# A value head's high and low parts side by side in one TensorE operand: weighing the values in a banded attention, in a two-layer transformer kernel

## The chip, the cores and the metric

One core of a Trainium2 chip runs the kernel as a single program. The metric is the device time of one execution in microseconds (us), median over runs. The engines are named as in the profile: PE (TensorE, matrix products; PEld is its weight load), DVE (VectorE), ACT (ScalarE), POOL (GpSimd) and SP (the queue that issues most DMAs). Each engine works through its own list of instructions in order; an instruction waits on semaphores for what it needs from other engines.

## The reference

Two layers on 512 tokens of width 1024, all in float32. Layer 0 has a differential attention, layer 1 a banded one; each layer ends in a gated feed-forward network. The change lies in the banded attention of layer 1:

```
def swa_sink_attention(h, cos, sin, w_q, q_norm, sinks, w_o, kw, vw):
    ...
    s = jnp.einsum('bnqhgd,bnkhd->bnhgqk', qb, kw).astype(jnp.float32) * (1.0 / math.sqrt(HEAD_DIM))
    ...
    m = jnp.maximum(jnp.max(s, axis=-1, keepdims=True), sink)
    e = jnp.exp(s - m)
    p = e / (jnp.sum(e, axis=-1, keepdims=True) + jnp.exp(sink - m))
    o = jnp.einsum('bnhgqk,bnkhd->bnqhgd', p.astype(vw.dtype), vw)
    return o.reshape(B, S, SW_HEADS * HEAD_DIM) @ w_o
```

There are 4 blocks of 128 queries, 4 value heads of 64 columns, and 4 query heads for each value head. A block of queries sees its own block of keys and the one before it; the first block has only its own.

## The kernel before

**Split products.** TensorE takes rounded operands (the type fp32r), so every float32 operand is split into a high part (a rounding cast on ACT, `split_evac` L298 or `split` L585) and a low part (the difference, on DVE, L299 or L587). `mm3` (L291 to L294) makes a product from three matmuls: high by high, high by low and low by high.

**Stages.** Pairs of heads of layer 0's attention, its feed-forward network (to about 605 us in the profile), the banded attention (about 605 to 785 us), the second feed-forward network (to the end). The order of PE's instructions is the order in which the program calls them (`manual_schedule` for PE). The other engines' orders come from a scheduler that works with priorities: `tc.high_priority` with a larger offset puts instructions forward.

**The banded attention.** It has 16 units, one for each block of queries and value head. A unit goes through `turn_q` (transpose the queries), `score` (products with the keys into two PSUM banks; DVE takes mask and maximum, L1388; ACT takes the exponentials, L1399, and scales them, L1406), `turn_p` (four transposes per key block on PE, L1418, then the split of the probabilities into `ph` on ACT, L298, and `pl` on DVE, L299) and `weigh`, the step that changes. When each step of a unit is issued on PE stands in a table written by hand, `SW_AT` (L117, five numbers per unit); between two steps, `Fill` puts in matmuls of the dense products that are due then (the projections of the queries, keys and values, later the output projection `o_sw`). This table is the same in both kernels.

**weigh before (L1424 to L1439).** The probabilities of a key block stand as 512 columns: 256 for the two even query heads, 256 for the two odd ones. The values lie in two padded tensors, `vpad[0]` (high) and `vpad[1]` (low), with 64 columns of zeros on either side of each head's 64. For the even heads the operand is taken so that the 64 value columns come first and zeros second, for the odd heads the other way round, and both are added into the same 256 columns of one PSUM bank `po`: partitions 0 to 63 hold the even heads and 64 to 127 the odd ones. Per key block that is 2 halves of `mm3`, six matmuls over 256 columns. Four units have one key block, twelve have two: 28 blocks. `po` then leaves through `split_evac` (L1438): ACT casts `oh` from PSUM, DVE subtracts `ol` from PSUM. There is one buffer for `po`, so the next unit's first matmul waits until both have read it. `oh` and `ol` are the operands of the output projection. The zeros of `vpad` are written once on POOL (two memsets, L1294), ahead of the rotation tables that POOL makes for this stage.

Of the kernel before, what the change touches and what calls it, by code (L numbers as in the profile page):

```python
# [17 lines left out]
P = 128  # L18
S = 512
NT = S // P  # L20
# [117 lines left out]
def tile_yoco_hybrid(  # L138
# [27 lines left out]
    def nm(s):  # L166
        count[0] += 1
        return f"{s}_{count[0]}"
# [1103 lines left out]
    with tc.tile_pool(name="sw", bufs=1, reuse_waits="tile") as ap:  # L1272
# [7 lines left out]
        maskS = maskD[:, 256:512]  # L1280
        vpad = [ap.tile([P, NT, 9, HD], F32R, name=nm("vpad"), tag=f"vpad{e}") for e in range(2)]
        kT = new_kT(ap, "kTs")
# [4 lines left out]
        def prepare():  # L1287
# [4 lines left out]
                                    compare_op=ALU.is_gt, fill=NEG, base=0, channel_multiplier=-1)  # L1292
            for e in range(2):
                nc.gpsimd.memset(vpad[e][:, :, 0::2, :].bitcast(F32), 0.0)  # L1294
            tables(Cs, Ss, gsw, HD, nc.gpsimd, nc.gpsimd)
# [35 lines left out]
        def b_post(pts):  # L1331

            ts["B"] = []
            for t in range(NT):
# [4 lines left out]
                src = heads(pts[t][:, 256:512])  # L1339
                dh = vpad[0][:, t, 1::2, :]  # L1340
                with tc.high_priority(offset=HOT):
                    nc.scalar.activation(dh, src, AF.Copy, scale=rx[:, t:t + 1])
                    nc.vector.scalar_tensor_tensor(vpad[1][:, t, 1::2, :], src, rx[:, t:t + 1], dh.bitcast(F32),
                                                   op0=ALU.mult, op1=ALU.subtract)
# [79 lines left out]
        def weigh(u):  # L1424
            s, i, kk, kv, blocks = place(u)
            nb = len(blocks)
            po = att("po")
            assert vdone
            for b, blk in enumerate(blocks):
                for e in range(2):  # L1430
                    c0 = (2 * kv + 1 - e) * HD
                    vf = [vpad[z][:, blk].rearrange("p a e -> p (a e)")[:, c0:c0 + P] for z in range(2)]
                    es = slice(e * 256, (e + 1) * 256)
                    mm3(po[:, 0:256], vf[0], vf[1], pT[u, b][0][:, es], pT[u, b][1][:, es],
                        b == 0 and e == 0, b == nb - 1 and e == 1)
            oh = ap.tile([P, 2, P], F32R, name=nm("oh"), tag="oh", bufs=OSW)
            ol = ap.tile([P, 2, P], F32R, name=nm("ol"), tag="ol", bufs=OSW)
            split_evac(oh, ol, po[:, 0:256].rearrange("p (h q) -> p h q", q=P))  # L1438
            o_all[kv, i] = (oh, ol)  # L1439
# [106 lines left out]
```

## Time and profile before

| what | value |
|---|---|
| three runs | 1122.22, 1124.5 and 1125.8 us, median 1124.5 us |
| the profiled execution, span from first to last instruction | 1121.8 us |
| granted TensorE clock over the whole span | 1.000 of full speed |
| PE busy over the span | 1101.6 us, 98% |
| DVE busy | 1008.4 us, 90% |
| ACT busy | 711.3 us, 63% |

The span is the profiled execution's own time; what lies around it isn't recorded. The median of the runs is 2.7 us above it.

A busy share is an average over stages. Views that show one stretch (busy time by windows, the timeline, the chain of waits) say which engine the others wait for in it. In the chain, each piece is the work that the next piece waited for, with the share of the time that no other work hides.

### The profile page before, as it was taken

The numbers are of one execution on the slowest core, as the hardware profiler recorded it, in microseconds if no ns is written. First come the engines' busy times: TensorE is split into PE (matmuls) and PEld (weight loads), VectorE is DVE, ScalarE is ACT, GpSimd is POOL, SyncE is SP. The second block draws the span as 40 slices with busy tenths as digits, with TensorE's granted clock in tenths as the row PEclk, the third lists the DMA queues.
The fourth block names the chain that finished last, engine by engine and source line by source line (L and its number), as shares of the span: only waits on it lengthen the run. The fifth ranks groups of instructions, "written<-read, shape, count | busy, mean of one in ns | idle before, by whom it ended". The sixth has DMA issues, their size and how long they took to land.

```text
span 1121.8 us, 20162 instructions
## 1 busy us (share of the span) xinstructions
PE 1101.6 (98%) x7206; PEld 978.3 (87%) x7206; DVE 1008.4 (90%) x2418; ACT 711.3 (63%) x1577; POOL 55.5 (5%) x76
## 2 busy tenths in 40 slices
PE   8999999999999999999999999999999999999998
PEld 6878888778989989989998778878989989998997
DVE  5979798979999899999998787988899999899997
ACT  6575756454555665675678499697555666566574
POOL 1100000000000010010003000000010000000000
PEclk9999999999999999999999999999999999999999
DMA  6312121124453434336124311120545247246213
GB/s 198 113 57 77 38 77 50 65 72 140 146 162 98 141 80 160 112 82 203 57 48 106 111 41 57 39 76 25 198 138 168 76 104 207 85 104 178 77 30 103
DMA packets 94085, 114.90 MB, mean 102 GB/s; under 512 B 5993, under 2 KB 70914, under 8 KB 93986
## 3 DMA queue, kind: packets, MB, share of 16 engines
q1 hardware_dynamic: 87216, 100.97, 28.1%
q0 software_dynamic: 6720, 12.65, 6.3%
q8 instruction: 56, 0.92, 0.3%
q14 instruction: 43, 0.35, 0.1%
q10 hardware_dynamic: 50, 0.01, 0.0%
HBM read 99.98 MB, written 2.10 MB: 91 GB/s over the span
## 4 chain that ended last, share of the span: by engine, by line
PE 77%; DVE 12%; ACT 6%; DMA 2%; issue 1%; SPq 1%; DVEq 0%; ACTq 0%
PE acc L721 16%; PE tr L721 10%; PE tr L809 9%; PE acc L809 8%; PE acc L292 8%; PE acc L294 8%; PE acc L293 8%; PE po L721 2%; PE tr L435 2%; ACT s L1399 2%; DVE hss L385 1%; ACT s L1406 1%; DVE lo L587 1%; DMA r<-in_w_gate_up_dram 1%; PE tr L310 1%
## 5 line engine op out<-in xcount | busy, mean ns | idle before, releaser
L585 ACT CAST hi<-r 128x512 fp32r<-128x512 f32 x160 | 98.9, 620 | 79.5 <-PE acc L721 35.8
L292 PE MATMUL acc<-hi,hTh 128*128 128x512 f32 (+1 forms) x352 | 132.9, 377 | 2.5 <-DVE vl L1022 1.4
L293 PE MATMUL acc<-lo,hTh 128*128 128x512 f32 (+1 forms) x352 | 124.1, 353 | 0.4 <-DVE lo L269 0.4
L294 PE MATMUL acc<-hi,hTl 128*128 128x512 f32 (+1 forms) x352 | 124.2, 353 | 0.1
L585 ACT CAST hi<-g 128x512 fp32r<-128x512 f32 x154 | 94.9, 618 | 40.8 <-PE acc L293 19.2
L587 DVE TENSOR_TENSOR lo<-r,hi 128x512 fp32r<-128x512 f32 x160 | 105.3, 692 | 6.1 <-ACT hi L585 5.8
L585 ACT CAST hi<-raw 128x512 fp32r<-128x512 f32 x108 | 66.9, 621 | 62.5 <-PE tr L721 18.2
L792 ACT CAST ah<-lf 128x256 fp32r<-128x256 f32 x154 | 61.1, 404 | 47.9 <-PE tr L809 16.0
L721 PE MATMUL acc<-hTh,lo 128*128 128x256 f32 x288 | 81.6, 283 | 0.0
L721 PE MATMUL acc<-hTl,hi 128*128 128x256 f32 x288 | 81.5, 283 | 0.0
L721 PE MATMUL acc<-hTh,hi 128*128 128x256 f32 x288 | 81.5, 283 | 0.0
L721 PE MATMUL acc<-tl,hi 128*128 128x256 f32 x288 | 81.2, 282 | 0.0
L721 PE MATMUL acc<-th,hi 128*128 128x256 f32 x288 | 81.1, 282 | 0.0
L721 PE MATMUL acc<-th,lo 128*128 128x256 f32 x288 | 81.1, 282 | 0.0
L268 ACT CAST hi<-raw 128x512 fp32r<-128x512 f32 x96 | 57.3, 619 | 33.9 <-PE acc L294 24.6
L292 PEld LDWEIGHTS acc<-hi,hTh 128*128 128x128 f32 x352 | 66.7, 190 | 13.4 <-issue 2.6
L587 DVE TENSOR_TENSOR lo<-g,hi 128x512 fp32r<-128x512 f32 x110 | 76.1, 692 | 1.5 <-ACT hi L585 1.4
L294 PEld LDWEIGHTS acc<-hi,hTl 128*128 128x128 f32 x352 | 66.5, 189 | 10.1 <-DVE hTl L907 0.7
L584 POOL DMA_DIRECT2D lo<-g x44 | 38.5, 976 | 716.4 <-ACT lo L583 372.3
L587 DVE TENSOR_TENSOR lo<-raw,hi 128x512 fp32r<-128x512 f32 x108 | 73.4, 692 | 0.0
L269 DVE TENSOR_TENSOR lo<-raw,hi 128x512 fp32r<-128x512 f32 x96 | 64.7, 688 | 9.4 <-ACT hi L268 8.9
L293 PEld LDWEIGHTS acc<-lo,hTh 128*128 128x128 f32 x352 | 66.9, 190 | 6.5 <-DVE lo L269 0.7
(280 smaller groups left out, 3644.7 us busy)
## 6 DMA issues: line engine op xcount, KB each, us to landing
r<-in_w_gate_up_dram SPq DMA_DIRECT2D x80, 512.0 KB, 5.0
g<-in_w_down_dram SPq DMA_DIRECT2D x88, 256.0 KB, 5.4
lo<-g POOLq DMA_DIRECT2D x44, 256.0 KB, 3.8
raw<-in_da_w_qkv_dram SPq DMA_DIRECT2D x30, 256.0 KB, 3.3
raw<-in_da_w_qkv_dram SPq DMA_DIRECT2D x8, 512.0 KB, 3.7
raw<-in_da_w_o_dram SPq DMA_DIRECT2D x8, 512.0 KB, 3.7
raw<-in_w_gate_up_dram SPq DMA_DIRECT2D x8, 512.0 KB, 3.7
raw<-in_sw_w_o_dram SPq DMA_DIRECT2D x8, 512.0 KB, 3.8
```

The source lines that it names most:

```text
L268: nc.scalar.copy(hi, part)
L269: nc.vector.tensor_tensor(lo, part, hi.bitcast(F32), op=ALU.subtract)
L292: nc.tensor.matmul(dst, sh, mh, start=start, stop=False)
L293: nc.tensor.matmul(dst, sh, ml, start=False, stop=False)
L294: nc.tensor.matmul(dst, sl, mh, start=False, stop=stop)
L435: nc.tensor.matmul(banks[c][:, cols], q[a][rows], k[b][rows], start=a + b == 0, stop=a == 1)
L584: nc.gpsimd.dma_start(out=lo.bitcast(F32), in_=src, accum_op=ALU.add)
L585: nc.scalar.copy(hi, src)
L587: nc.vector.tensor_tensor(lo, src, hi.bitcast(F32), op=ALU.subtract)
L721: nc.tensor.matmul(dst, l[:, k, :], r[:, k, :], start=fresh and k == 0 and i == 0, stop=k == 3 and i == 2, skip_group_check=not fresh)
L792: nc.scalar.copy(ah, src)
L809: nc.tensor.matmul(bank, l[:, tk], r, start=fresh and i == 0 and n == 0, stop=i == len(qs) - 1 and n == 2, skip_group_check=not fresh)
```

## The change

The two padded tensors become one, `vv`, in which the 64 columns of a head's high part and the 64 of its low part stand side by side: 128 columns with no zeros. `weigh` takes this as the one operand, and streams all 512 columns of the high probabilities past it, then all 512 of the low ones: two matmuls per key block, in place of six. `po` now fills a whole bank: partitions 0 to 63 hold the sums with the high part, 64 to 127 those with the low part, and the columns hold the even heads and then the odd ones. (The product low by low, which `mm3` leaves out, is now in the sum.)

Since a head's two halves lie on different partitions, they are added behind the matmuls: ACT copies the lower half (64 partitions, 512 columns) to SBUF as `ocor`, and DVE adds it to the upper half in two additions of 256 columns into `osum`, the first for partitions 0 to 63 (even heads), the second for partitions 64 to 127 (odd heads). The split into `oh` and `ol` then reads `osum` in SBUF. `po` is free when the second addition has read it. `osum` and `ocor` have two buffers each. The two memsets on POOL are gone.

```diff
-        vpad = [ap.tile([P, NT, 9, HD], F32R, name=nm("vpad"), tag=f"vpad{e}") for e in range(2)]
+        vv = ap.tile([P, NT, 4, 2, HD], F32R, name=nm("vv"), tag="vv")
...
-            for e in range(2):
-                nc.gpsimd.memset(vpad[e][:, :, 0::2, :].bitcast(F32), 0.0)
...
-                dh = vpad[0][:, t, 1::2, :]
+                dh = vv[:, t, :, 0, :]
...
-                    nc.vector.scalar_tensor_tensor(vpad[1][:, t, 1::2, :], src, rx[:, t:t + 1], dh.bitcast(F32),
+                    nc.vector.scalar_tensor_tensor(vv[:, t, :, 1, :], src, rx[:, t:t + 1], dh.bitcast(F32),
...
             for b, blk in enumerate(blocks):
-                for e in range(2):
-                    c0 = (2 * kv + 1 - e) * HD
-                    vf = [vpad[z][:, blk].rearrange("p a e -> p (a e)")[:, c0:c0 + P] for z in range(2)]
-                    es = slice(e * 256, (e + 1) * 256)
-                    mm3(po[:, 0:256], vf[0], vf[1], pT[u, b][0][:, es], pT[u, b][1][:, es],
-                        b == 0 and e == 0, b == nb - 1 and e == 1)
+                v = vv[:, blk, kv].rearrange("p z e -> p (z e)")
+                for z in range(2):
+                    nc.tensor.matmul(po, v, pT[u, b][z], start=b == 0 and z == 0, stop=b == nb - 1 and z == 1)
...
-            split_evac(oh, ol, po[:, 0:256].rearrange("p (h q) -> p h q", q=P))
+            osum = ap.tile([P, 256], F32, name=nm("osum"), tag="osum", bufs=2)
+            ocor = ap.tile([P, 512], F32, name=nm("ocor"), tag="ocor", bufs=2)
+            with tc.high_priority(offset=pri["evac"]):
+                nc.scalar.copy(ocor[0:HD, :], po[HD:P, :])
+                for e in range(2):
+                    es = slice(e * 256, (e + 1) * 256)
+                    nc.vector.tensor_tensor(osum[e * HD:(e + 1) * HD, :], po[0:HD, es], ocor[0:HD, es], op=ALU.add)
+            split_evac(oh, ol, osum.rearrange("p (h q) -> p h q", q=P))
```

How the instructions stand on PE around the first unit's `weigh`, before. `acc` is a bank of a dense product, `tr` a bank of scores, and `po` the bank of the weighed values:

```order
L294 MATMUL acc_8354<-hi_8319,hTl_7565 128x512
L292 MATMUL po_8398<-ph_8167,vpad_7623 128x256
L293 MATMUL po_8398<-pl_8168,vpad_7623 128x256
L294 MATMUL po_8398<-ph_8167,vpad_7624 128x256
L292 MATMUL po_8398<-ph_8167,vpad_7623 128x256
L293 MATMUL po_8398<-pl_8168,vpad_7623 128x256
L294 MATMUL po_8398<-ph_8167,vpad_7624 128x256
L435 MATMUL tr_8411<-kTs_7625,q_8382 128x256
```

The same place on PE in the changed kernel:

```order
L294 MATMUL acc_8351<-hi_8316,hTl_7565 128x512
L1430 MATMUL po_8395<-ph_8164,vv_7623 128x512
L1430 MATMUL po_8395<-pl_8165,vv_7623 128x512
L435 MATMUL tr_8409<-kTs_7624,q_8379 128x256
L435 MATMUL tr_8410<-kTs_7624,q_8379 128x256
```

Six matmuls over 256 columns have become two over 512, and what stands around them on PE has not moved; this holds at all 28 blocks.

The end of the stage on ACT, before. `oh_9883` and `oh_9929` belong to the last two units, `hi` is a cast of feed-forward weights, `hTh` a cast of the transposed tokens of the feed-forward network, `xn` the squares for its norm:

```order
L522 ACTIVATE xn_9889,fss_9888<-xs 128x1024
L298 CAST ph_9866<-tr_9861 128x512
L298 CAST oh_9883<-po_9870 128x256
L298 CAST ph_9912<-tr_9907 128x512
L298 CAST oh_9929<-po_9916 128x256
L268 CAST hi_10010<-raw_10008 128x512
L268 CAST hi_10014<-raw_10008 128x512
L298 CAST hTh_9615<-tr_9940 128x4x128
L298 CAST hTh_9615<-tr_9947 128x4x128
```

The same place on ACT in the changed kernel (`oh_9846` and `oh_9889` are the last two units'):

```order
L298 CAST ph_9837<-tr_9832 128x512
L522 ACTIVATE xn_9857,fss_9856<-xs 128x1024
L1436 COPY ocor_9849<-po_9841 64x512
L298 CAST ph_9880<-tr_9875 128x512
L298 CAST oh_9846<-osum_9848 128x256
L1436 COPY ocor_9892<-po_9884 64x512
L268 CAST hi_9975<-raw_9973 128x512
L268 CAST hi_9979<-raw_9973 128x512
L298 CAST hTh_9592<-tr_9905 128x4x128
L298 CAST hTh_9592<-tr_9912 128x4x128
L298 CAST oh_9889<-osum_9891 128x256
```

Each unit's cast is now two instructions, the copy first; the last unit's cast has moved behind two weight casts and two token casts.

The same stretch on DVE, before (`L249` and `L528` belong to the norm of the third group of tokens, `L269` to the feed-forward weights):

```order
L249 SCALAR_TENSOR_TENSOR frr_9892<-rsq_t_9894,rsq_s_9893 128x1
L528 SCALAR_TENSOR_TENSOR xn_9889<-xs,frr_9892,gb_9278 128x512
L528 SCALAR_TENSOR_TENSOR xn_9889<-xs,frr_9892,gb_9280 128x512
L299 TENSOR_TENSOR ol_9930<-po_9916,oh_9929 128x256
L269 TENSOR_TENSOR lo_10011<-raw_10008,hi_10010 128x512
```

And in the changed kernel:

```order
L249 SCALAR_TENSOR_TENSOR frr_9860<-rsq_t_9862,rsq_s_9861 128x1
L1439 TENSOR_TENSOR osum_9891<-po_9884,ocor_9892 64x256
L528 SCALAR_TENSOR_TENSOR xn_9857<-xs,frr_9860,gb_9259 128x512
L528 SCALAR_TENSOR_TENSOR xn_9857<-xs,frr_9860,gb_9261 128x512
L1439 TENSOR_TENSOR osum_9891<-po_9884,ocor_9892 64x256
L299 TENSOR_TENSOR hTl_9593<-tr_9905,hTh_9592 128x4x128
L299 TENSOR_TENSOR ol_9890<-osum_9891,oh_9889 128x256
```

The last unit's two additions stand on either side of the norm's two multiplications, and its subtraction behind the first low part of the tokens.

## The prediction

> **What bounds the kernel now.** I read the page first, for the span and its chain of waits, then the busy time by windows over the stage that changes, then the chain of waits in that stage alone, and last the timeline at single places.
>
> ```profile
> span 1121.8 us, 20162 instructions
> ```
>
> Over the whole program the chain lies mostly on PE:
>
> ```profile
> PE 77%; DVE 12%; ACT 6%; DMA 2%; issue 1%; SPq 1%; DVEq 0%; ACTq 0%
> ```
>
> That average covers feed-forward stages in which nothing changes. The units' `weigh` steps run from 666 to 777 us. The busy time there, in six stretches (columns: length, then PE, PEld, DVE, ACT, POOL with instruction counts):
>
> ```profile
> 660.00:680.00 20.00, 18.64 (x125) 15.69 (x123) 18.62 (x76) 17.95 (x50) 0.00 (x0) 1.00 0.14 41
> 680.00:700.00 20.00, 20.00 (x132) 16.14 (x131) 13.76 (x57) 17.91 (x54) 0.00 (x0) 1.00 0.20 66
> 700.00:720.00 20.00, 19.35 (x121) 16.24 (x120) 19.16 (x65) 12.41 (x32) 1.14 (x2) 1.00 0.19 54
> 720.00:740.00 20.00, 20.00 (x134) 15.85 (x133) 16.57 (x66) 18.12 (x61) 0.00 (x0) 1.00 0.09 27
> 740.00:760.00 20.00, 19.59 (x127) 15.56 (x126) 16.33 (x58) 17.26 (x46) 0.00 (x0) 1.00 0.26 80
> 760.00:780.00 20.00, 19.00 (x118) 15.54 (x117) 17.20 (x59) 16.16 (x43) 0.00 (x0) 1.00 0.00 0
> sum 120.00, PE 116.57 PEld 95.03 DVE 101.64 ACT 99.81 POOL 1.14; mean PE 19.43 PEld 15.84 DVE 16.94 ACT 16.64 POOL 0.19
> ```
>
> PE is busy for 116.6 of 120 us, but DVE for 101.6 and ACT for 99.8: three engines near their limits, in a stage where a unit passes from one to the other five times. The chain of waits for 655 to 785 us, by line, shows which of them sets the pace:
>
> ```profile
> by line: ACT s L1399 12.2%; ACT s L1406 8.7%; PE acc L292 8.6%; PE acc L293 7.9%; PE acc L294 7.9%; PE tr L435 4.3%; PE tr L1418 3.7%; ACT ph L298 3.3%; ACT hi L268 3.3%; PE po L292 3.0%; issue 2.6%; PE po L293 2.6%; PE po L294 2.6%; DVE lo
> ```
>
> The exponentials and scalings on ACT lead it. In its order of time (start, us, what), the last units look like this:
>
> ```profile
> 766.12 1.71 ACT s L1406 x4
> 767.82 2.34 ACT s L1399 x8
> 770.26 0.48 ACT ph L298
> 770.76 1.71 ACT s L1406 x4
> 772.47 0.47 ACT ph L298
> ...
> 775.39 0.34 DVE ol L299
> ```
>
> From 766 to 773 us ACT goes from one piece to the next without a gap, and PE's matmuls are the ones that fit in. PE works all the time, and yet for half of this stage its work is not what the end waits for.
>
> **What is removed on PE.** The number of blocks comes from the group of the first of the three matmuls, and the pace from the timeline at the fourteenth unit:
>
> ```profile
> L292 PE MATMUL po<-ph,vpad 128*128 128x256 f32 x56 | 16.7, 299 | 1.4 <-DVE ol L299 0.8 <-DVE hss L386 0.7
> ```
>
> ```profile
> 763.59 0.28 PE L293 MATMUL po<-pl,vpad 128*128 128x256 f32 x1
> ...
> 764.90 0.40 PE L292 MATMUL acc<-hi,oh 128*128 128x512 f32 x1
> ...
> 767.66 0.60 PE L1418 MATMUL tr<-ident,s 128*128 128x128 f32 x4
> ```
>
> Two of these per block, 56 in all, make 28 blocks and 168 matmuls. From 763.59 to 764.90 us there are eleven steps of 256 columns, 0.119 us each; from 764.90 to 767.66 twelve of 512, 0.230 us each. (The printed durations overlap; the steps are what PE needs.) A block goes from 6 x 0.119 = 0.714 to 2 x 0.230 = 0.460 us, so 0.254 us less. Over 28 blocks PE loses 7.1 of 20.0 us of work.
>
> The Trainium skill, "TensorE: Matmul & The Clock Gate", section "Back-to-back issue gap", gives a step as the columns over 2.4 GHz plus 2.5 ns: 109 ns for 256 columns and 216 ns for 512. By it the 28 blocks would save 6.2 us. The trace's steps are 9% and 7% longer, and I go by them.
>
> Only what lies on the path counts. In the chain by line, the three `po` groups have 3.0 + 2.6 + 2.6 = 8.2% of 130 us, 10.7 of the 20.0 us. So 10.7 x 0.254 / 0.714 = **3.8 us** come off the path; the other 3.3 us come off PE where it is ahead of ACT and DVE, and are worth nothing unless these keep up.
>
> **What is added on ACT and DVE.** The rows nearest to the new instructions, with the old ones first. They are the casts and subtractions of `po`, a copy of 512 columns from PSUM, an addition of 256 columns with one operand in PSUM, and a cast of 256 columns from SBUF:
>
> ```profile
> L298 ACT CAST oh<-po 128x256 fp32r<-128x256 f32 x16 | 5.8, 363 | 2.7 <-PE po L294 2.4
> L299 DVE TENSOR_TENSOR ol<-po,oh 128x256 fp32r<-128x256 f32 x16 | 6.6, 413 | 0.7 <-ACT oh L298 0.5
> L792 ACT CAST ah<-lf 128x256 fp32r<-128x256 f32 x154 | 61.1, 404 | 47.9 <-PE tr L809 16.0 <-PE acc L809 9.7 <-DVE lf L739 8.5
> ```
>
> ```profile
> L1121 ACT COPY osb<-po x8: 564/587/588, 76.5 to 244.6; 128x512 f32<-128x512 f32 x8
> ```
>
> ```profile
> L737 DVE TENSOR_TENSOR uc<-uc,po x18: 412/416/422, 350.9 to 1083.7; 128x256 f32<-128x256 f32 x18
> ```
>
> No row of before has 64 partitions instead of 128 with these columns; I take the durations as they stand, since the columns set them in every row above (363 and 587 ns on ACT for 256 and 512). Behind another instruction a piece shows less than its duration, because its start lies beside its predecessor's end: 0.48 us for a 512-column cast from PSUM and 0.34 for a 256-column subtraction, both in the chain above. So ACT gets 0.48 to 0.59 us more per unit for the copy and 0.04 for the cast from SBUF (404 against 363 ns), at 0.52 us 8.3 us over 16 units. DVE gets two additions, 0.68 us if they start in the shadow of their predecessors and 0.83 if not, 10.9 to 13.3 us. The subtraction stays at 413 ns.
>
> Here the Trainium skill has a rule against the change. "VectorE: DVE Perf Modes", section "Two Vector instructions with no wait between them", says in a model that an instruction whose output starts in another quarter of the partitions than the output before it starts only when all earlier ones have finished. The second addition writes from partition 64, so by the rule it and the instruction behind it would lose the shadow, and 0.83 us would hold, 13.3 us in all, rather than 10.9. No run here shows such an output yet.
>
> On the path, seven of the sixteen evacuations appear as pieces of the chain: three casts on ACT and four subtractions on DVE, the first and the last being
>
> ```profile
> 698.62 0.26 ACT oh L298
> ...
> 775.39 0.34 DVE ol L299
> ```
>
> Three get a copy in front (3 x 0.52 = 1.6 us), four get two additions (4 x 0.76, the middle of 0.68 and 0.83, = 3.0 us): **4.6 us**. Bounds: nothing, if the scheduler's new order puts them into gaps that ACT and DVE have (20 and 18 us in the 120), and 16 x (0.52 + 0.76) = 20.5 us if every unit waits for both.
>
> **The end of the stage.** The last unit's `oh` and `ol` are needed at once. PE, ACT and DVE there:
>
> ```profile
> 775.77 0.39 PE L292 MATMUL po<-ph,vpad 128*128 128x256 f32 x1 [0.76 <-DVE ol L299]
> ...
> 777.31 0.40 PE L292 MATMUL acc<-hi,oh 128*128 128x512 f32 x1
> ...
> 779.50 0.48 PE L292 MATMUL acc<-hi,oh 128*128 128x512 f32 x1
> ```
>
> ```profile
> 777.51 0.37 ACT L298 CAST oh<-po 128x256 fp32r<-128x256 f32 x1 [1.88 <-PE po L294]
> 778.21 1.31 ACT L268 CAST hi<-raw 128x512 fp32r<-128x512 f32 x2 [0.32 <-PE acc L294]
> 779.43 1.07 ACT L298 CAST hTh<-tr 128x512 fp32r<-128x512 f32 x2
> ```
>
> ```profile
> 777.30 1.41 DVE L528 SCALAR_TENSOR_TENSOR xn<-xs,frr,gb 128x512 f32<-128x512 f32 x2
> 778.63 0.42 DVE L299 TENSOR_TENSOR ol<-po,oh 128x256 fp32r<-128x256 f32 x1
> ```
>
> The last `weigh` gives way to the first output product at 777.31 us; call it E. PE needs the last `oh` at 779.50, E + 2.2, and has it since E + 0.6. In the new order ACT copies from E + 0.2 to E + 0.8, DVE makes the first addition to E + 1.2, then both multiplications of the norm to E + 2.6, then the second addition to E + 2.9. On ACT the cast of `oh` stands behind two weight casts and the two token casts, which can't end before E + 3.2 (now 780.50), and so ends at E + 3.6. PE stalls for 3.6 - 2.2 = **1.4 us** in front of the last products. The only `po` buffer is also freed later: copy and two additions (0.59 + 0.76) in place of cast and subtraction (0.36 + 0.41), 0.6 us more where the next unit follows closely, as at 775.77; I count this within the pieces above.
>
> **On POOL.** The memsets lie here:
>
> ```profile
> 605.42 2.28 POOL L1294 MEMSET vpad<- 128x1280 f32 x2 [7.61 <-PE acc L809]
> ```
>
> ```profile
> L403 DVE TENSOR_TENSOR td<-t,Cs x8: 683/690/693, 627.8 to 724.4; 128x512 f32<-128x512 f32 x8
> ```
>
> They stand ahead of the tables `Cs` and `Ss`, but these are first read 20 us after the memsets end. Worth nothing. SP's issues keep their order, and the new tensors take less memory than the old.
>
> **The sum.** By the path: -3.8 + 4.6 + 1.4 = +2.2 us. A second count, without the path: in each of the six stretches take the busiest engine after the change, with 5, 3, 6, 2, 6 and 6 of the 28 blocks off PE (0.254 each) and 3, 2, 2, 3, 2 and 4 evacuations on ACT (0.52) and DVE (0.68 to 0.83). The largest are DVE 20.7 to 21.1, PE 19.2, DVE 20.5 to 20.8, ACT 19.7, ACT 18.3 and DVE 19.9 to 20.5: together 118.3 to 119.7 against 120, so -1.7 to -0.3 us. The first count leaves no room for work to shift into gaps, the second no room for waits between the engines. I take the middle of +2.2 and -0.3, which is +1.0: on the median of the three runs, **1125.5 us**. A change below 0.3% (3.4 us) is about what a measurement of this kernel can't tell from none.
>
> **Rivals.**
> *The gain on PE is kept.* ACT has 20 and DVE 18 us of gaps in the 120, some of them spent waiting for PE (the 1.88 above), and these shrink when PE comes earlier. If all copies and additions fit there, what is left is -7.1 + 1.4 = -5.7 us: 1118.8. Against it stands the unbroken run of ACT pieces above. Chance of more than 3.4 us faster: 0.24.
> *The additions hold up the next units.* DVE and ACT take their lists in order. A first addition at the head of DVE's list waits for the copy, which waits behind exponentials on ACT; behind it on DVE stand the next unit's maxima (L1388) and `pl`, for which ACT and PE wait. Each evacuation on the path then costs copy and additions, 1.28 us. With n of them the sum is 1.28 n - 3.8 + 1.4; it passes +3.4 us from n = 5, and with 8 of 16 it is +7.8: 1132.3. For it: 93% of DVE and 90% of ACT in 660 to 680 us are taken already. Against it: PE stalled for only 3.4 of the 120 us, and a PE that comes earlier by 0.25 to 0.5 us per unit also starts the next unit's chain earlier. Chance: 0.30.
> That the change does less than it says can be left out: the order shows 56 matmuls in place of 168.
>
> **How the numbers follow.** No measurable change is the likeliest, 0.46, with its own range from 1121.1 to 1127.9. The range of 8 in 10 reaches into both others: down to 1119 (nearly all of PE's gain kept) and up to 1131.5 (nearly half of the evacuations at full price on the path).
>
> **What would show it.** In the profile of the changed kernel: steps of 0.23 us for the new matmuls, and 7 us less PE work in `po`; the copy at about 0.59 us x16 and the addition at about 0.42 us x32; PE idle in 660 to 780 us up from 3.4 to near 11 us, with ACT `ph`, `s` and DVE `osum` named as what ended it; a stall of 1 to 2 us before the last `oh`. It is wrong if PE's idle time there stays at 3 us (then the gain was kept), or if the chain shows `ocor` and `osum` in most of the units.

## The result, and the profile after

The changed kernel takes 1149.2 us (median of four; 1146.8 to 1149.9) against 1124.5 us for the kernel before on the same chip. The ratio is 1.0223, with a 95% interval of 1.0205 to 1.024: 25 us slower, against a forecast of 1125.5 us and a range to 1131.5 us. The forecast was wrong in size, and no change was the wrong outcome.

The profiled execution took 1146.8 us. Its page begins:

```profile
span 1144.6 us, 19995 instructions
```

The two traces start the first unit's weighing 0.15 us apart (666.15 and 666.30 us). The first feed-forward matmul behind the stage starts at 784.57 us before and at 808.06 us after, 23.5 us later, and from there to the end both take the same time within 1 us (337.2 and 336.5), so the whole loss lies in the stage that was changed. The busy time in the same stretches of 20 us as in the prediction, and one more (columns: length, PE, PEld, DVE, ACT, POOL with instruction counts, then PE's granted clock, DMA share and GB/s):

```profile
660.00:680.00 20.00, 18.27 (x99) 13.34 (x98) 18.42 (x76) 18.87 (x52) 0.00 (x0) 1.00 0.09 27
680.00:700.00 20.00, 18.35 (x118) 14.16 (x117) 14.44 (x57) 16.40 (x49) 0.00 (x0) 1.00 0.16 54
700.00:720.00 20.00, 15.59 (x67) 11.13 (x64) 16.90 (x50) 15.80 (x38) 0.60 (x1) 0.83 0.20 67
720.00:740.00 20.00, 18.93 (x114) 14.00 (x112) 17.46 (x69) 11.74 (x40) 0.54 (x1) 1.00 0.06 14
740.00:760.00 20.00, 15.85 (x93) 11.00 (x93) 16.53 (x58) 18.48 (x51) 0.00 (x0) 0.99 0.31 93
760.00:780.00 20.00, 17.12 (x93) 12.94 (x92) 14.67 (x49) 14.73 (x41) 0.00 (x0) 0.92 0.04 13
780.00:800.00 20.00, 14.29 (x56) 10.78 (x55) 13.88 (x51) 12.97 (x32) 0.00 (x0) 0.84 0.00 1
```

Look at all three engines at once. In 660 to 780 us (the first six rows) PE falls from 116.6 to 104.1 us, but DVE falls too, from 101.6 to 98.4, and ACT from 99.8 to 96.0, although each unit now gives both more to do: fewer units pass in the same time. No engine has become the full one; all three wait more. And the clock column, 1.00 throughout before, drops to 0.83, 0.92 and 0.84.

From 660 us to the first feed-forward matmul, the kernel before and the changed one:

```profile
660.00:784.57 124.57, 121.14 (x770) 98.86 (x769) 105.88 (x384) 103.07 (x288) 1.14 (x2) 1.00 0.16 48
```

```profile
660.00:808.06 148.06, 125.23 (x657) 92.81 (x657) 119.23 (x416) 113.61 (x304) 1.14 (x2) 0.94 0.12 38
```

PE's idle time goes from 124.57 - 121.14 = 3.4 to 148.06 - 125.23 = 22.8 us, and its busy time rises by 4.1 us, although 7.1 us of work were taken away. What ended the waits (total us, times, longest), first before, then after:

```profile
PE tr L1418 <- DVE mx L1388: 1.4, 1, 1.4
PE po L292 <- DVE ol L299: 0.8, 1, 0.8
```

```profile
PE po L1430 <- DVE osum L1439: 7.0, 3, 4.0
PE acc L292 <- ACT oh L298: 6.8, 3, 2.8
PE tr L1416 <- DVE mx L1386: 4.7, 4, 2.7
```

Two of the three largest are the new way from `po` to `oh`: PE waits for the buffer `po` until the second addition has read it, and the output products wait for `oh`. The new instructions themselves have the durations that were forecast, and so does their number:

```profile
L1439 DVE TENSOR_TENSOR osum<-po,ocor 64x256 f32<-64x256 f32 x32 | 13.3, 414 | 4.5 <-ACT ocor L1436 4.2
L1436 ACT COPY ocor<-po 64x512 f32<-64x512 f32 x16 | 9.3, 583 | 3.9 <-PE po L1430 3.5
```

The longest wait shows how they cost more than they last. It is the same unit, the sixth, in both kernels. Before, its matmuls end at 703.5 us; ACT and DVE:

```profile
706.22 0.64 ACT L384 ACTIVATE sq<-t 128x512 f32<-128x512 f32 x1
706.74 0.37 ACT L298 CAST oh<-po 128x256 fp32r<-128x256 f32 x1
...
707.58 0.39 DVE L299 TENSOR_TENSOR ol<-po,oh 128x256 fp32r<-128x256 f32 x1
```

After, they end at 705.2 us; ACT, DVE and PE:

```profile
708.79 1.16 ACT L384 ACTIVATE sq<-t 128x512 f32<-128x512 f32 x2
...
709.84 1.70 ACT L1404 ACTIVATE s<-s,rs 128x256 f32<-128x256 f32 x4
711.57 0.58 ACT L1436 COPY ocor<-po 64x512 f32<-64x512 f32 x1
...
712.18 0.85 DVE L1439 TENSOR_TENSOR osum<-po,ocor 64x256 f32<-64x256 f32 x2 [1.30 <-ACT ocor L1436]
...
713.10 0.39 ACT L298 CAST oh<-osum 128x256 fp32r<-128x256 f32 x1
713.17 0.77 PE L1430 MATMUL po<-ph,vv 128*128 128x512 f32 x1 [4.03 <-DVE osum L1439]
```

The copy stands on ACT behind squares and scalings of other units and starts 6.4 us after its data were there; DVE then waits 1.3 us for it with the additions at the head of its list, and PE 4.0 us for DVE. Unit by unit, from the end of the last weighing matmul to the end of `ol`, the timelines give a mean of 2.35 us before and 5.33 us after (16 units each). That is 3.0 us more per unit, where the added instructions last 0.58 + 0.83 = 1.4 us. The rest is standing in ACT's and DVE's lists: `evac_hot`, below, puts these instructions forward in the lists, and the mean falls to 3.36 us.

**The clock.** After some waits of PE the granted clock is halved for a stretch of 3.41 us. These are the five such stretches (clock column 0.50), each run of them with the stretch before it. The rows from 766.41 to 773.24 us are for comparison: PE was idle for half of the first of them, and the clock stayed at 1.00.

```profile
708.42:711.83 3.41, 0.72 (x4) 0.24 (x2) 2.11 (x6) 3.39 (x8) 0.00 (x0) 1.00 0.37 122
711.83:715.24 3.41, 1.78 (x3) 0.79 (x3) 3.02 (x7) 2.25 (x5) 0.00 (x0) 0.50 0.17 65
715.24:718.66 3.42, 3.33 (x9) 2.34 (x10) 3.36 (x15) 1.23 (x3) 0.60 (x1) 0.50 0.13 42
```

```profile
756.17:759.58 3.41, 0.79 (x6) 0.75 (x7) 3.07 (x12) 3.39 (x11) 0.00 (x0) 1.00 0.68 194
759.58:763.00 3.42, 3.42 (x11) 2.63 (x10) 3.17 (x9) 3.01 (x8) 0.00 (x0) 0.50 0.32 113
766.41:769.83 3.42, 1.72 (x9) 1.07 (x8) 2.14 (x11) 2.94 (x7) 0.00 (x0) 1.00 0.00 0
769.83:773.24 3.41, 2.23 (x12) 1.35 (x14) 3.31 (x12) 2.22 (x6) 0.00 (x0) 1.00 0.01 2
783.48:786.89 3.41, 1.57 (x6) 1.00 (x7) 2.80 (x8) 2.91 (x11) 0.00 (x0) 1.00 0.00 0
786.89:790.31 3.42, 3.42 (x14) 2.83 (x13) 1.38 (x2) 1.92 (x5) 0.00 (x0) 0.50 0.00 0
793.72:797.13 3.41, 1.04 (x7) 0.78 (x6) 2.78 (x10) 2.72 (x6) 0.00 (x0) 1.00 0.01 2
797.13:800.55 3.42, 3.42 (x10) 2.56 (x9) 2.76 (x9) 1.21 (x2) 0.00 (x0) 0.50 0.02 5
```

PE is busy for 1.78 + 3.33 + 3 x 3.42 = 15.4 us at half clock, work that takes about half as long at full clock: in the stretch from 786.89 us a matmul of 512 columns takes a step of 0.43 us, behind it 0.23. So up to 7.7 us of the loss are this, and they are the larger part of why PE's busy time rose: it is -7.1 + 7.7 + 3.5 us. Some of these 3.5 us are matmuls that print longer behind a wait; the rest I can't assign.

### The profile page after: what moved, and what is told of

Read it like the earlier page. It is cut to its first block, busy times and chain, and to the rows that moved or that the text cites. A ratio compares the mean times of both kernels' runs of the same rounds, so it can differ in the third digit from the quotient of the medians.

```text
span 1144.6 us, 19995 instructions
## 1 busy us (share of the span) xinstructions
PE 1106.8 (97%) x7094; PEld 972.1 (85%) x7094; DVE 1024.8 (90%) x2450; ACT 723.8 (63%) x1593; POOL 54.3 (5%) x74
## 4 chain that ended last, share of the span: by engine, by line
PE 76%; DVE 12%; ACT 7%; DMA 3%; issue 1%; SPq 1%; DVEq 0%; ACTq 0%
PE acc L721 18%; PE tr L721 11%; PE tr L809 9%; PE acc L809 8%; PE acc L292 7%; PE acc L294 7%; PE acc L293 7%; PE po L721 2%; ACT s L1397 2%; PE tr L435 2%; DVE lo L269 1%; ACT s L1404 1%; DVE hss L385 1%; PE po L809 1%; DVE u L401 1%
## 5 line engine op out<-in xcount | busy, mean ns | idle before, releaser
L292 PEld LDWEIGHTS acc<-hi,hTh 128*128 128x128 f32 x352 | 66.7, 190 | 13.6 <-issue 2.6
L269 DVE TENSOR_TENSOR lo<-raw,hi 128x512 fp32r<-128x512 f32 x96 | 64.5, 684 | 12.3 <-ACT hi L268 12.1
```

What stands on the lines that cost most here:

```text
L269: nc.vector.tensor_tensor(lo, part, hi.bitcast(F32), op=ALU.subtract)
L292: nc.tensor.matmul(dst, sh, mh, start=start, stop=False)
```

## The experiments

Four theories, and the expectations name two narrower ones where they need them. HOPS: the loss is the longer chain from `po` to `oh`, four crossings between engines instead of two. WORK: it is the time that ACT and DVE spend on the new instructions. HOLD: it is `po`, the single buffer, held until the second addition. ORDER: it is the new order of ACT's and DVE's lists, which the scheduler makes anew for each kernel. Ratios are to the kernel before on the same chip, with 95% intervals; 0.001 is 1.1 us.

**The two halves of the change apart.** The new matmuls with the old evacuation, `gain_alone`:

```diff
-            split_evac(oh, ol, osum.rearrange("p (h q) -> p h q", q=P))
+            split_evac(oh, ol, po[:, 0:256].rearrange("p (h q) -> p h q", q=P))
```

(and without the lines of `ocor` and `osum`).

> The new matmuls, but oh and ol are made straight from the first 256 columns of po as before the change: no copy ocor, no additions osum (so the low part's halves are left out of the result). What it tells: what PE's side of the change is worth when ACT and DVE get nothing new. Theory HOPS (the loss comes from the longer way from po to oh, ACT, DVE, ACT, DVE, which PE waits for) and theory WORK (the loss comes from the 0.59 us of copy and 0.83 us of additions per unit that ACT and DVE have no time for) expect the same here: 3.8 to 7.1 us less than before, 1117.4 to 1120.7 us. If it comes out at before's time or above, the matmuls themselves, or the order that they lead to, cost time, and both theories miss a part.

1129.3 us, ratio 1.004 (1.0021 to 1.0059). Less work on PE and nothing added, and the kernel is 4 to 5 us slower: both theories missed a part.

The old matmuls with the new evacuation, `evac_alone`:

```diff
-            split_evac(oh, ol, po[:, 0:256].rearrange("p (h q) -> p h q", q=P))
...
+                nc.scalar.copy(ocor[0:HD, :].rearrange("p (e c) -> p e c", e=2),
+                               po[HD:P, 0:256].unsqueeze(1).to_broadcast([HD, 2, 256]))
+                for e in range(2):
+                    es = slice(e * 256, (e + 1) * 256)
+                    nc.vector.tensor_tensor(osum[e * HD:(e + 1) * HD, :], po[0:HD, 0:256], ocor[0:HD, es], op=ALU.add)
+            split_evac(oh, ol, osum.rearrange("p (h q) -> p h q", q=P))
```

> The other half of the change alone: the six matmuls of 256 columns per block as before, and behind them the new way from po to oh, with the copy of 512 columns (the 256 columns that there are, read twice), the two additions, the cast and the subtraction, so that the result holds sums of heads that don't belong together. Theory HOPS and theory WORK as they stand, with the matmuls' part and the evacuation's part independent: 1149.2 - 1129.3 = 19.9 us on top of before, 1142 to 1147 us. Theory BOTH (the loss needs a PE that comes earlier and finds po and oh not ready): clearly less, 1126 to 1137 us, because PE's own 7.1 us of work cover part of the wait.

1147.7 us, ratio 1.0204 (1.0183 to 1.0226), 0.7 us above the first range. The evacuation alone makes a loss as large as the whole change's, with PE's work as before. BOTH falls.

**The order.** The kernel before and `gain_alone`, each with another priority for evacuations, `before_order` and `gain_order`:

```diff
-SW_EVAC = 30
+SW_EVAC = 28
```

> The kernel before with one number changed: the scheduler's priority for evacuations in this stage is 28 instead of 30. PE's list is the same; some 48 of ACT's 1306 and 82 of DVE's 2382 rows stand elsewhere, no work is added or removed. Theory ORDER (the stage is fitted so closely that any other order of the same work costs several us, and that is why gain_alone is slower than before): 1128 to 1135 us. If the order alone is worth little: 1122.5 to 1127 us.

1129.5 us, ratio 1.0043 (1.0026 to 1.006): the same work, in another order on ACT and DVE, costs 5 us.

```diff
-SW_EVAC = 30
+SW_EVAC = 32
```

> gain_alone (the new matmuls, the old evacuation; the low part left out) with the scheduler's priority for evacuations at 32 instead of 30: PE's list stays, some 35 of ACT's 1306 and 90 of DVE's 2380 rows stand elsewhere. Theory ORDER (before_order's 5 us show that a list that isn't the fitted one costs about that; gain_alone paid it too and hid PE's gain under it): the times of such lists scatter, 1121 to 1133 us, and a value below 1124 would show that some of the 7.1 us can be had. Theory NO GAIN (the stage is set by ACT and DVE, PE's lighter matmuls are worth nothing in any order): 1127 to 1133 us.

1131.8 us, ratio 1.0086 (1.0064 to 1.0107). Both theories allowed for this; it tells nothing.

To take the order out, ACT's and DVE's lists were pinned row by row, by edges of order (they make nobody wait for data). `LISTS` holds the numbers of the instructions in the order of the kernel whose lists are wanted:

```diff
+    def pin(engine, first, total, rows):
+        ins = [i for i in nc.cur_bb.bb.instructions if str(i.engine).endswith(engine)]
...
+        for p, q in zip(rows, rows[1:]):
+            tc.add_manual_dep(ins[q], ins[p].name, info, reason="pin")
+
+    for engine, first, total, rows in LISTS:
+        pin(engine, first, total, rows)
```

`gain_pinned` is `gain_alone` with the lists of before: in its trace all 1577 instructions of ACT and all 2418 of DVE stand in the order of before. `before_gainlists` is the kernel before with the lists of `gain_alone`.

> gain_alone (the new matmuls, the old evacuation, the low part left out) with ACT's and DVE's lists pinned row for row to those of the kernel before, so that PE's lighter matmuls are the only difference. Theory ORDER (PE's saving is real, and the scheduler's new lists took it back): 1117 to 1121.5 us. Theory NO GAIN (ACT and DVE set the stage; the saving only turns into waits of PE): 1122 to 1126 us. Slower than 1127 us would mean that lighter matmuls cost time by themselves.

1121.9 us, ratio 0.997 (0.9959 to 0.9982). Its median lies between the two ranges, 0.4 us above the first and 0.1 below the second, but the kernel before took 1125.2 us on this chip: 3.4 us are saved (2.0 to 4.6).

> The kernel before with ACT's and DVE's lists pinned to those that the scheduler made for gain_alone: 80 of ACT's and 181 of DVE's rows stand elsewhere, and all work and PE's list are those of before. ORDER: the lists are what costs, 1128 to 1134 us. If lists and PE's pace only fit together (these lists are good for the faster PE and bad for nothing): 1122 to 1127 us.

1131.0 us, ratio 1.0056 (1.0037 to 1.0075). ORDER holds for this part: the lists cost 6 us by themselves, without a half-clock stretch in the stage, and they had hidden PE's saving. In `gain_pinned` the stage, up to the first feed-forward matmul, is

```profile
660.00:784.22 124.22, 117.43 (x668) 89.11 (x669) 106.27 (x387) 103.83 (x293) 1.14 (x2) 1.00 0.15 48
```

PE is busy for 3.7 us less and idle for 6.8 instead of 3.4 us: half of the work taken away turns into waiting. (This execution came to the first unit's matmuls 1.8 us later than that of the kernel before, and left the stage 0.35 us earlier, so the stage took 2.1 us less in it. It had a half-clock stretch at 20.3 us, long before the stage.)

The changed kernel with the lists of before, `after_pinned`: the copies stand where the casts of `oh` stood and the additions where the subtractions stood; cast and subtraction stand two rows later.

> The changed kernel with ACT's and DVE's lists pinned to those of before and the new instructions set in: each copy where the cast of oh stood and the cast two rows later, both additions where the subtraction stood and the subtraction two rows later. Nothing is left out. ORDER: what the scheduler's lists cost goes (5 us or more), 1136 to 1144 us. HOPS and WORK alone, without a part for the lists: 1146 to 1152 us. A time at or below that of before would need PE's saving and a cheap evacuation at once; I don't expect it.

1147.3 us, ratio 1.0197 (1.0181 to 1.0214), against 1.0223 (1.0205 to 1.024) for the scheduler's own lists. ORDER is no large part of the changed kernel's loss: its own lists cost (1.0223 - 1.0197) x 1124.5 = 2.9 us, and the two intervals overlap. Between `gain_pinned` and `after_pinned` only the evacuation differs: (1.0197 - 0.997) x 1124.5 = 25.5 us. So the whole change is -3.4 us for PE, +25.5 for the evacuation and +2.9, not clear of the noise, for the order: 25 us in all.

**Where the evacuation's price comes from.** All new instructions, but their result is read by nobody, `work_aside`, whose edit this is; and the same with a constant table as their input, `work_free`:

```diff
+            split_evac(oh, ol, po[:, 0:256].rearrange("p (h q) -> p h q", q=P))
...
-            split_evac(oh, ol, osum.rearrange("p (h q) -> p h q", q=P))
```

> All instructions of the change, but oh and ol are made straight from the first 256 columns of po, and the copy ocor and the additions osum stand behind them with a result that nobody reads (so the low part is left out of the result). ACT and DVE have all the new work, and po is held until the second addition, but nobody waits for oh longer than before. HOPS: the work alone costs little, the most of the 24.7 us loss is gone: 1121 to 1131 us. WORK: the same work, the same loss, 1141 to 1150 us.

1142.1 us, ratio 1.0157 (1.0134 to 1.018): in WORK's range and far above HOPS'. But what PE waited for was mostly `po`, until `osum` had read it, hence the next one:

```profile
PE po L1430 <- DVE osum L1440: 12.3, 6, 4.0
PE tr L1416 <- DVE mx L1386: 2.5, 2, 1.7
```

> As work_aside, but the copy and the two additions that nobody reads take a table in SBUF that never changes in place of po, so that ACT and DVE have the same number of instructions with the same columns while po is free again after the subtraction (the low part is left out of the result). If work_aside's 12.9 us over gain_alone come from po being held until the second addition (theory HOLD: one buffer, for which the next unit's matmuls wait): 1129 to 1134 us. If they come from the time that ACT and DVE need (theory WORK): 1138 to 1143 us.

1135.5 us, ratio 1.0097 (1.0076 to 1.0118), between the two ranges. ACT's copies waited 6.0 us for a free `ocor` in it, a wait that the experiment itself brought in, so it doesn't divide HOLD from WORK cleanly.

The chain with little work, `hops_small`:

```diff
-                nc.scalar.copy(ocor[0:HD, :], po[HD:P, :])
+                nc.scalar.copy(ocor[0:HD, 0:16], po[HD:P, 0:16])
...
-                    es = slice(e * 256, (e + 1) * 256)
-                    nc.vector.tensor_tensor(osum[e * HD:(e + 1) * HD, :], po[0:HD, es], ocor[0:HD, es], op=ALU.add)
+                    es = slice(e * 8, (e + 1) * 8)
+                    nc.vector.tensor_tensor(osum[e * HD:(e + 1) * HD, 0:8], po[0:HD, es], ocor[0:HD, es], op=ALU.add)
```

> The way from po to oh keeps all its steps (ACT copy, two DVE additions, ACT cast, DVE subtraction, each waiting for the one before), but the copy has 16 columns instead of 512 and each addition 8 instead of 256; osum is a fixed pair of buffers cleared once (so the result is left out but for 8 columns). HOPS: most of the loss stays, less only the length of the pieces (at most 1.0 us per unit where they are on the path): 1133 to 1146 us. WORK: ACT and DVE get almost nothing, and the gain of the matmuls shows: 1118 to 1126 us.

1137.0 us, ratio 1.0103 (1.0072 to 1.0135), as HOPS had it.

Since each of these has lists of its own, the two halves were repeated with the lists of before, `work_pinned` (`work_free`, no wait for `ocor` now: 0.4 us) and `hops_pinned`:

> gain_pinned with the copy and the two additions of every unit added on a table that never changes, each set right behind the cast or the subtraction of the old evacuation (nobody waits for their result, po isn't held, the low part is left out). Against gain_pinned's 1121.9 us: WORK (each copy and addition pushes back what follows, 1.28 us for every evacuation that is on the path): 1132 to 1142 us. HOPS (ACT and DVE have gaps enough, and only the waiting counts): 1122 to 1128 us.

1135.8 us, ratio 1.0112 (1.0097 to 1.0127), as WORK had it.

> hops_small with the lists of before: the full chain from po over ocor, osum and oh to ol, with a copy of 16 columns and additions of 8, cast and subtraction each two rows later in the lists (the result is left out but for 8 columns). Against gain_pinned's 1121.9 us: HOPS: most of after_pinned's 25 us, 1134 to 1144 us. WORK: 1122 to 1128 us.

1139.7 us, ratio 1.0147 (1.0131 to 1.0163), as HOPS had it. Against `gain_pinned` the work that nobody waits for costs (1.0112 - 0.997) x 1124.5 = 16.0 us and the chain of short pieces 19.9 us. Each theory expected the other's half to be cheap, and each is wrong there: both are real. They come to 35.9 us where the full evacuation costs 25.5, so they overlap. In part that is because the second half isn't free of work: a copy of 16 columns still lasts 0.17 us and an addition of 8 columns 0.15, 0.5 us per unit against 1.4. That a wait for one hides some of the other is likely, but not shown by itself. PE's largest waits in `work_pinned`, then in `hops_pinned` (their line numbers stand 4 and 7 above those of the changed kernel):

```profile
PE po L1434 <- DVE ol L303: 3.0, 2, 1.5
PE tr L1420 <- DVE mx L1390: 3.0, 3, 1.6
```

```profile
PE acc L296 <- ACT oh L302: 4.2, 4, 2.2
PE po L1437 <- DVE osum L1446: 3.2, 2, 1.8
```

With the work alone, what comes late is the old evacuation's `ol` and the next unit's maxima; with the chain alone, `oh` and `osum`.

**Ways out.** The five instructions of the evacuation at a high priority, so that they stand earlier in the two lists, `evac_hot`:

```diff
-            with tc.high_priority(offset=pri["evac"]):
+            with tc.high_priority(offset=HOT):
```

(and the cast and the subtraction likewise).

> The changed kernel in full; only the five instructions from po to ol get the scheduler's high priority (1220 in place of 30), so that they stand earlier in ACT's and DVE's lists. HOPS, in the form that the way is long because its pieces stand behind others in the two lists: a good part of the loss is gone, 1125 to 1138 us. WORK: the same pieces in another order, the loss stays within 4 us: 1145 to 1153 us.

1147.2 us, ratio 1.0206 (1.0181 to 1.023): in WORK's range, and HOPS' is missed by 9 us. The way itself did get shorter: from the last weighing matmul to the end of `ol` it takes 3.36 us on the mean, against 5.33 in the changed kernel and 2.35 before. But moving its pieces ahead pushes back the rest, and PE now waits for scalings, maxima and a `ph` instead:

```profile
PE tr L1416 <- ACT s L1404: 5.5, 5, 2.6
PE tr L1416 <- DVE mx L1386: 4.4, 3, 3.1
PE po L1430 <- ACT ph L298: 4.3, 1, 4.3
```

A copy of all of `po`, read by the additions, so that `po` is free after one instruction, `po_early`:

```diff
-                nc.scalar.copy(ocor[0:HD, :], po[HD:P, :])
+                nc.scalar.copy(ocor, po)
...
-                    nc.vector.tensor_tensor(osum[e * HD:(e + 1) * HD, :], po[0:HD, es], ocor[0:HD, es], op=ALU.add)
+                    nc.vector.tensor_tensor(osum[e * HD:(e + 1) * HD, :], ocor[0:HD, es], ocor[HD:P, es], op=ALU.add)
```

> The changed kernel, but the copy on ACT takes all 128 partitions of po instead of the lower 64, and the additions read both halves from this copy: po is free after one instruction on ACT, and the length of every step and their number stay. HOLD: what PE waits for po (7.0 us in the changed kernel, and two stretches of half clock behind it, 5.1 us) goes, 1137 to 1142 us. HOPS or WORK without a part for po: 1146 to 1151 us.

1148.2 us, ratio 1.0211 (1.0188 to 1.0234), in the range of HOPS and WORK.

The late units' sums in free banks, `po_acc`:

```diff
-            po = att("po")
+            po = acc() if u >= 10 else att("po")
```

> The changed kernel, but from the eleventh unit on the weighted sums go into the four banks of acc, which only the output products still use by then, instead of the single po. ACT's and DVE's lists differ in some 10 rows, so that this is nearly the same order. HOLD: what the late units wait for po goes, the 2.4 us in front of the last unit and the half clock behind it (1.7 us): 1143 to 1147 us. HOPS (it is oh that is late; po is only the first to be waited for): the wait turns up in front of the output products, 1147 to 1150 us.

1146.6 us, ratio 1.0211 (1.0195 to 1.0226): inside HOLD's range, but its interval overlaps that of the changed kernel. The 2.4 us that PE waited for `po` ahead of the last unit became

```profile
796.74 0.50 PE L1430 MATMUL acc<-ph,vv 128*128 128x512 f32 x1 [1.04 <-ACT ph L298]
798.00 0.80 PE L1430 MATMUL acc<-pl,vv 128*128 128x512 f32 x1 [0.76 <-DVE pl L299]
803.47 0.51 PE L292 MATMUL acc<-hi,oh 128*128 128x512 f32 x1 [1.18 <-ACT oh L298]
```

With both, HOLD falls as a cause of its own in the changed kernel: `po` is only where PE meets the late ACT and DVE first. (Where `po` is held longest, in `work_aside`, holding it may cost up to the (1.0157 - 1.0097) x 1124.5 = 6.7 us that lie between it and `work_free`; their lists differ too.)

One of four scalings on POOL, in the changed kernel and in the one before, `after_pool` and `before_pool`:

```diff
-                nc.scalar.activation(sb[:, g, 0:n], sb[:, g, 0:n], AF.Copy, scale=rs[:, g:g + 1])
+                if g < 3:
+                    nc.scalar.activation(sb[:, g, 0:n], sb[:, g, 0:n], AF.Copy, scale=rs[:, g:g + 1])
+                else:
+                    nc.gpsimd.tensor_scalar(sb[:, g, 0:n], sb[:, g, 0:n], rs[:, g:g + 1], None, op0=ALU.mult)
```

> The changed kernel with one of the four scalings of the probabilities per unit on POOL, which has nothing else to do here, instead of ACT: ACT gets rid of 0.43 us per unit, 6.9 us in all, nearly what the copy costs it. WORK as far as ACT is meant: 1140 to 1145 us. HOPS: the way from po to oh is the same, 1145 to 1152 us. If POOL's instruction takes longer than the three that stay on ACT (1.3 us), the units' own chain gets longer, and it is slower than 1152 us.

1147.5 us, ratio 1.0212 (1.0192 to 1.0231): taking 6.9 us off ACT returns next to nothing. (A scaling lasts 0.85 us on POOL, less than the three that stay on ACT.)

> The kernel before with the same step on POOL, no matmul and no evacuation changed. If ACT's time bounds the stage, as the chain of before has it: up to 6.9 us less, 1117 to 1122 us. If the fitted order is worth more than ACT's time: 1124 to 1131 us.

1125.7 us, ratio 1.0014 (1.0004 to 1.0023). The same there: ACT's busy time in 660 to 780 us falls from 99.8 to 92.0, and the time stays. That the exponentials and scalings on ACT lead the chain of waits before did not make ACT's time the bound.

The cast to `oh` on DVE, so that the chain crosses twice less, with pinned lists, `two_hops_pinned`:

```diff
-            split_evac(oh, ol, osum.rearrange("p (h q) -> p h q", q=P))
+                osv = osum.rearrange("p (h q) -> p h q", q=P)
+                nc.vector.tensor_copy(oh, osv)
+                nc.vector.tensor_tensor(ol, osv, oh.bitcast(F32), op=ALU.subtract)
```

> The changed kernel in full, with the cast of osum to oh on DVE instead of ACT: the way from po goes over ACT once and then stays on DVE (two additions, cast, subtraction), two crossings between engines less; ACT's list is that of before with the copy in the place of the cast, DVE's that of before with additions and cast ahead of the subtraction. ACT has 0.36 us per unit less to do than in the changed kernel, DVE a cast of 256 columns more. HOPS: a third to a half of the loss goes, 1133 to 1141 us. WORK (DVE is the fuller engine): 1145 to 1155 us.

1143.2 us, ratio 1.0171 (1.0154 to 1.0188), between the ranges. Two crossings less gain about 3 us against `after_pinned`, though DVE gets 4.7 us more to do; the two intervals overlap a little, so the 3 us are not firm. It is the fastest form of the whole change that was run, and still 19 us slower than before. No version with the full result beats the kernel before.

## Why the prediction was wrong

**The failed step** is the price of the evacuation: "On the path, seven of the sixteen evacuations appear as pieces of the chain", at 0.52 us for a copy and 0.76 for two additions, 4.6 us in all. With equal lists it was 25.5 us, above even the bound of 20.5 us that the step gave for all sixteen. The outcome was the one to which the prediction gave 0.30. Three things in the step were wrong:

- *Which units pay.* The count took the pieces that lay on the path of the kernel before. But the units that were off it did not stay off it. In the chain of waits after, `ocor` or `osum` stand in at least eleven of the sixteen units (the prediction named "most of the units" as the sign that it is wrong).
- *What a unit pays.* The step priced durations (1.28 us). The work that nobody waits for costs 16.0 us, 1.0 per unit, so the gaps of 20 us on ACT and 18 on DVE, taken as possible cover, did not take it up. The longer chain costs as much by itself (19.9 us, with short pieces), and in the sum its new crossings had no price at all: at each one a piece stands in a list behind other units' work. Nor can the price be moved away: with the pieces ahead in the lists (`evac_hot`) the others stand behind them, and the loss stays.
- *The clock.* The bound assumed PE at full clock. In this trace four stretches of 3.41 us in which PE was more than half idle (0.72, 0.79, 1.57 and 1.04 us busy) are followed by half clock, so that these waits are in part paid a second time. This is up to 7.7 us of the changed kernel's loss, read from the trace; no experiment varied it alone.

**PE's saving** was sized rightly: 3.8 us forecast, 3.4 us (2.0 to 4.6) measured with the lists of before, and about half of the 7.1 us turned into waiting, as forecast. That the two numbers lie so close is in part luck: with the lists of `gain_alone` the same matmuls save (1.0056 - 1.004) x 1124.5 = 1.8 us, inside the noise. And the step left out that the scheduler makes new lists when PE's work changes; those of `gain_alone` cost 6 us (`before_gainlists`), those of the changed kernel about 3, not clear of noise. The prediction read the order only for what stands where, not as a term with a price.

**The second count**, by the busiest engine in each stretch, gave -0.3 to -1.7 us and was the worse guide: it takes engines as independent, and after the change none of them is busy for over 19 of the 20 us in any stretch.

**The end of the stage**: forecast was 1.4 us of stall ahead of the last products, measured 1.24 us, on `oh`, as forecast:

```profile
802.92 0.51 PE L292 MATMUL acc<-hi,oh 128*128 128x512 f32 x1 [1.24 <-ACT oh L298]
```

What the step called "0.6 us more where the next unit follows closely" was a wait of 2.37 us for `osum` ahead of the last unit.

**The rival** "the additions hold up the next units" had the right mechanism, ACT's and DVE's lists taken in order, with the right places (`po`, maxima, `pl`). Its size, 1132.3 us, came from the same price of 1.28 us and n = 8. Its argument against, that PE stalled for only 3.4 of 120 us, did not hold: that PE rarely waited before said nothing of how much it would wait behind a longer chain. PE's idle time in 660 to 780 us, which the prediction put near 11 us, became 120 - 104.1 = 15.9.

**The sizes** held: 583 ns for the copy, 414 for the addition; steps of 0.23 to 0.24 us for the new matmuls, so about 0.5 us less on PE for a unit of two blocks; POOL's memsets were worth nothing that was seen. The two additions take 0.85 us at 712.18, without a shadow. In the chain of waits a first addition shows 0.33 us behind another instruction and the second, which writes from partition 64, 0.43:

```profile
674.25 0.33 DVE osum L1439
674.75 0.43 DVE osum L1439
```

In all sixteen units the second addition and the instruction behind it start after the end of the one before them; nine of the first additions start 0.08 us ahead of it. By the rule of the Trainium skill that the prediction weighed ("VectorE: DVE Perf Modes", section "Two Vector instructions with no wait between them") it is the second that starts late; the trace agrees.

**Open** is how the 25.5 us divide exactly, since work and chain overlap by 10 us and the clock has a part in both. In the profiled executions PE was busy at half clock in this stage for 19.3 us in `after_pinned`, 13.6 in `hops_pinned`, 9.2 in `work_pinned` and not at all in `gain_pinned`, so up to half of these times belongs to the clock. Open is also PE's own order. In every run here PE takes its steps in the order of the table `SW_AT` of the kernel before, and whether a table that leaves the longer chain more time would lower the price was not run.

## What to carry to other kernels

When a step in a pipeline of engines gets more instructions and more crossings, don't price it by the pieces that lie on the path of the kernel before. Here these came to 4.6 us, all sixteen units at full price to 20.5, and the measured price was 25.5. The delay from a step's input to its last output is a sign of trouble (3.0 us more per unit, for 1.4 us of added work) but not the price either: `evac_hot` took two thirds of that delay away and won nothing that is clear of the noise, because other pieces waited instead. Where PE, ACT and DVE are 97, 85 and 83% busy and feed each other, as here, take a longer chain as paid by nearly every unit. And when a scheduler makes the order, pin the old one before judging a small gain: here it turned +4.5 into -3.4 us.

## What the runs showed of the hardware

- The half-clock stretches start and end on a grid of 3.41 us: in the changed kernel at 711.8, 759.6, 786.9 and 797.1 us, 14, 8 and 3 grid steps apart. In it, stretches in which PE was busy for 0.72, 0.79, 1.04 and 1.57 us were followed by half clock, those with 1.72 and 2.23 us were not. Busy time alone isn't the rule: in `work_pinned` one with 2.64 us was followed by half clock too:

```profile
676.49:679.90 3.41, 2.64 (x20) 1.71 (x19) 2.87 (x9) 2.43 (x6) 0.00 (x0) 1.00 0.36 126
679.90:683.31 3.41, 2.34 (x9) 1.58 (x7) 2.79 (x15) 1.25 (x4) 0.00 (x0) 0.50 0.10 33
```

  The Trainium skill ("TensorE: Matmul & The Clock Gate", section "What's actually happening") has the same window, 3413 ns and free-running, and the halved clock after an idle window of about 3.4 us. The windows agree; that a window must be idle does not, and the measurement decides: PE half idle in it, and once less, was enough.
- A copy on ACT of 64 partitions lasts as long as one of 128: 583 and 577 ns for 512 columns from PSUM (the changed kernel and `po_early`).
